# Layer 0 of a two-layer encoder: where the modulation steps stand around the start of the output projection

## The chip, the cores and the metric

The kernel runs on one core of a Trainium2 chip. The metric is the device time of one launch in microseconds (us). Each time is the median of several runs. The engines are TensorE (PE, with PEld for its weight loads), VectorE (DVE), ScalarE (ACT), GpSimd (POOL) and SyncE (SP), which issues nearly all transfers.

## What is computed

A trunk of two layers over 256 tokens of width 2048, all in 32-bit floats. In each layer a vector `c` gives six modulation vectors. The normalised input goes through one input projection whose columns feed four groups (A to D), their outputs are joined and go through the output projection `w_out`, and a gated feed-forward network follows.

```python
mod = (c_act @ w_mod[l] + b_mod[l]).reshape(bn, 6, d)
shift_m, scale_m, gate_m = mod[:, 0, None], mod[:, 1, None], mod[:, 2, None]
...
h = layer_norm(x) * (1.0 + scale_m) + shift_m
proj = h @ w_in[l]
uv, q_c, kv_c, k_r, sb, sc, sh, ag = jnp.split(proj, IN_SPLITS, axis=-1)
y_a = gmlp_mixer(...)          # A
y_b = mla_mixer(...)           # B: latent attention
y_c = short_conv_mixer(...)    # C: short convolution
y_d = conformer_conv(...)      # D: 31 taps, layer norm over channels, swish
y = jnp.concatenate([y_a, y_b, y_c, y_d], axis=-1) @ w_out[l]
x = layer_norm(ALPHA * x + (1.0 + gate_m) * y, post_mix_g[l], post_mix_b[l])
h = layer_norm(x) * (1.0 + scale_f) + shift_f
y = conv_ffn(h, ...)
x = layer_norm(ALPHA * x + (1.0 + gate_f) * y, post_ffn_g[l], post_ffn_b[l])
```

## The kernel before

**Products.** TensorE sets the time. A weight block is loaded by SP into a `raw` tile (128 x 2048 floats, 1 MB), ScalarE casts it to a high half `whi` (L414) and VectorE subtracts to get the low half `wlo` (L423), 1024 columns at a time. Three products then replace one exact product. The input projection of layer 0 and the first two units of its output projection skip the split: their weights are loaded straight into `wexact` tiles (L398), and TensorE does each of their products in two passes.

**Modulation steps.** One step is a 1 MB load of a block of `w_mod` into a `raw` tile (`wmod`, L201, on SP) and one VectorE instruction over 128 x 2048 (L205). There are 192 in all, and they need nothing but `c`, so they are strewn between the other work. `pump` does this: each unit of products adds a rate to a credit, and each whole credit draws one step. The rates stand in `RATES`, by layer and phase: `C` is the short-conv group, `out` the first chunk of the output projection, `out_next` the second, `out_tail` the first two units of the third.

**Buffers.** `wmod` and `wraw` tiles share four buffers and take them in turn. So the load of a tile waits on SP until VectorE is done with the tile four earlier, and SP issues in order: a load behind a waiting one waits too. `wexact`, `whi` and `wlo` tiles share eight others, which TensorE's products release.

**The stage around the change.** Group C of layer 0 has eight units of 1 MB, and `run` loads two units ahead, so the last two units issue no load of their own. In them `pump` still draws steps. Then the output projection (`out_proj`) takes the 2048 output columns in three chunks: 1024 (eight units u0 to u7 of 24 split products, u0 and u1 exact), 512 (four units) and 512 (four units). In the third chunk all products of token tile 0 come first, 48 of them, then 48 of tile 1. While TensorE does those of tile 1, the other engines finish and normalise tile 0 (L703 to L783, then `xn`), and TensorE turns the result (`ps_xT`, L649).

**Group D's norm** runs in between: TensorE sums the channels (`ps_mean`) and the squares (`ps_var` from `sqD`), VectorE and GpSimd make a reciprocal deviation (`rd`, L1010; L153; `dgD`, L1016), TensorE spreads it (`ps_rD`), VectorE scales `convD` by it (L1027) and ScalarE applies the swish (`yd`, L1029) and casts (`a`, L444). In layer 1 the same norm runs around the last unit of group E, just ahead of the output projection.

**Order.** The program is written as above, but the order of instructions on each engine is made by a scheduler from its own estimate of durations. So an edit of the rates also moves instructions that it does not name.

## Time and profile before

| | us |
|---|---|
| median of 3 runs | 2199.75 (2199.68 to 2200.93) |
| the profiled execution, its time | 2200.61 |
| the profiled execution, its span | 2198.8 |
| TensorE busy in the span | 2171.1 |
| VectorE busy | 1740.1 |
| ScalarE busy | 1100.8 |

The span runs from the first to the last instruction; 1.8 us lie around it. Times inside the trace count from the start of the span. Group C of layer 0 ends at about 289 us, the output projection of layer 0 runs to about 390 us, and group E of layer 1 ends at about 1361 us. A row of the timeline gives start, duration, engine, line, operation, `out<-in`, and a count of merged instructions; in brackets stands the idle time before and what ended it. A matmul's duration is its latency; how fast they follow each other is read from counts.

### The profile page before, as it was taken

The numbers are of one execution on the slowest core, as the hardware profiler recorded it, in microseconds if no ns is written. First come the engines' busy times: TensorE is split into PE (matmuls) and PEld (weight loads), VectorE is DVE, ScalarE is ACT, GpSimd is POOL, SyncE is SP. The second block draws the span as 40 slices with busy tenths as digits, with TensorE's granted clock in tenths as the row PEclk, the third lists the DMA queues.
The fourth block names the chain that finished last, engine by engine and source line by source line (L and its number), as shares of the span: only waits on it lengthen the run. The fifth ranks groups of instructions, "written<-read, shape, count | busy, mean of one in ns | idle before, by whom it ended". The sixth has DMA issues, their size and how long they took to land. (4 is left out here: it accounts for less than half of the span.)

```text
span 2198.8 us, 28486 instructions
## 1 busy us (share of the span) xinstructions
PE 2171.1 (99%) x10916; PEld 1806.8 (82%) x10916; DVE 1740.1 (79%) x2325; ACT 1100.8 (50%) x1686; POOL 21.2 (1%) x40
## 2 busy tenths in 40 slices
PE   8999999999999999999999999999999999999997
PEld 6776868688888888888868988868888888888886
DVE  5658999789889889889978989977777755565777
ACT  3133644655555455545574545465544544454553
POOL 0000000000000000000000000000000000000000
PEclk9999999999999999999999999999999999999999
DMA  9999988688999888988768647956766655565553
GB/s 390 416 377 390 366 332 335 235 333 309 331 333 338 330 330 331 358 324 286 290 230 324 206 151 294 342 218 243 262 248 246 224 190 188 189 211 192 196 197 141
DMA packets 94907, 617.08 MB, mean 281 GB/s; under 512 B 10737, under 2 KB 10929, under 8 KB 27441
## 3 DMA queue, kind: packets, MB, share of 16 engines
q1 hardware_dynamic: 94466, 614.70, 75.6%
q8 instruction: 85, 1.39, 0.2%
q0 software_dynamic: 176, 0.53, 0.1%
q14 instruction: 52, 0.43, 0.1%
q10 hardware_dynamic: 128, 0.03, 0.0%
HBM read 613.08 MB, written 2.13 MB: 280 GB/s over the span
## 5 line engine op out<-in xcount | busy, mean ns | idle before, releaser
L414 ACT CAST whi<-wraw 128x1024 fp32r<-128x1024 f32 (+1 forms) x620 | 643.8, 1046 | 683.5 <-PE g_c L121 196.0
L423 DVE TENSOR_TENSOR wlo<-wraw,whi 128x1024 fp32r<-128x1024 f32 (+1 forms) x620 | 742.9, 1213 | 278.6 <-ACT whi L414 260.8
L121 PE MATMUL v_c<-hT,whi 128*128 128x512 f32 x1408 | 489.6, 392 | 0.0
L205 DVE SCALAR_TENSOR_TENSOR wmod<-wmod,crep 128x2048 f32<-128x2048 f32 x192 | 438.4, 2286 | 60.3 <-DMA wmod<-in_w_mod_dram 59.4
L121 PE MATMUL g_c<-hT,whi 128*128 128x512 f32 x1280 | 444.6, 391 | 0.0
L121 PE MATMUL v_c<-hT,wlo 128*128 128x256 f32 x1408 | 395.1, 281 | 0.0
L121 PE MATMUL d<-whi,a 128*128 128x512 f32 x1344 | 386.7, 390 | 0.0
L121 PE MATMUL g_c<-hT,wlo 128*128 128x256 f32 x1280 | 358.8, 280 | 0.0
L121 PEld LDWEIGHTS v_c<-hT,whi 128*128 128x128 f32 x1408 | 263.8, 187 | 57.0
L121 PEld LDWEIGHTS d<-whi,a 128*128 128x128 f32 x1344 | 252.2, 188 | 52.3
L121 PEld LDWEIGHTS g_c<-hT,whi 128*128 128x128 f32 x1280 | 239.8, 187 | 51.9
L121 PEld LDWEIGHTS v_c<-hT,wlo 128*128 128x128 f32 x1408 | 266.4, 189 | 0.4 <-DVE wlo L423 0.4
L121 PEld LDWEIGHTS g_c<-hT,wlo 128*128 128x128 f32 x1280 | 242.2, 189 | 0.0
L121 PE MATMUL d<-wlo,a 128*128 128x512 f32 x672 | 233.1, 389 | 0.0
L121 PEld LDWEIGHTS d<-wlo,a 128*128 128x128 f32 x672 | 126.2, 188 | 26.2
L121 PE MATMUL o<-whi,a 128*128 128x512 f32 x416 | 120.5, 390 | 0.0
L121 PEld LDWEIGHTS o<-whi,a 128*128 128x128 f32 x416 | 77.9, 188 | 16.5 <-ACT whi L414 0.4
L448 DVE TENSOR_TENSOR a<-g,a 128x512 fp32r<-128x512 f32 x132 | 87.7, 684 | 0.0
L592 PE MATMUL first<-wexact,hN 128*128 128x512 f32 x192 | 85.5, 596 | 0.3
L444 ACT CAST a<-g 128x512 fp32r<-128x512 f32 x132 | 76.9, 614 | 0.0
L121 PE MATMUL o<-wlo,a 128*128 128x512 f32 x208 | 72.7, 393 | 1.9 <-DVE wlo L423 1.8
L1569 DVE SCALAR_TENSOR_TENSOR u<-g,par,u 128x254 f32<-128x254 f32 (+1 forms) x176 | 74.2, 477 | 0.2
(316 smaller groups left out, 2144.6 us busy)
## 6 DMA issues: line engine op xcount, KB each, us to landing
wmod<-in_w_mod_dram SPq DMA_DIRECT2D x192, 1024.0 KB, 7.1
wraw<-in_ffn_w_up_dram SPq DMA_DIRECT2D x168, 1024.0 KB, 5.4
wraw<-in_ffn_w_down_dram SPq DMA_DIRECT2D x88, 1024.0 KB, 5.0
wexact<-in_w_in_dram SPq DMA_DIRECT2D x64, 512.0 KB, 12.3
wraw<-in_w_out_dram SPq DMA_DIRECT2D x30, 1024.0 KB, 6.5
wraw<-in_w_in_dram SPq DMA_DIRECT2D x24, 1024.0 KB, 5.5
wexact<-in_ffn_w_up_dram SPq DMA_DIRECT2D x16, 512.0 KB, 5.4
wlate<-in_late_dram SPq DMA_DIRECT2D x8, 1024.0 KB, 7.1
```

The lines of the kernel that those rows point to most:

```text
L121: i = pe.matmul(o, lhsT, rhs, start=start, stop=stop, skip_group_check=True)
L205: i = dve.scalar_tensor_tensor(out=raw, in0=raw, scalar=1.0, in1=crep, op0=ALU.mult, op1=ALU.mult, accum_out=col)
L414: i = act.copy(hi[:, :m], r)
L423: i = dve.tensor_tensor(out=lo[:, :m], in0=r, in1=hi[:, :m].bitcast(F32), op=ALU.subtract)
L444: i = act.copy(hi, src)
L448: dve.tensor_tensor(out=lo, in0=src, in1=hi.bitcast(F32), op=ALU.subtract)
L592: i = pe.matmul(ps, hN[kt // 4][:, kt % 4, t * P : (t + 1) * P], parts[kt], start=kt == 0, stop=kt == KT - 1, skip_group_check=True,)
L1569: dve.scalar_tensor_tensor(out=u[:, sh:], in0=x[:, : S - sh], scalar=col(k, j), in1=u[:, sh:], op0=ALU.mult, op1=ALU.add)
```

## The change

Two edits, both on the pump. `run` sets `held` while it is in the last `ahead` units of a group, and a held pump draws nothing but keeps the credit. A pump now draws at most two steps a call. Only group C of layer 0 is run with `ahead` over 0, so only its last two units are held. The rates of layer 0's output projection are set anew: 0.75 instead of 1.0 a unit in the first chunk, 0.25 instead of 0 in the second, 1.0 instead of 0.5 in the first two units of the third.

```diff
-    dict(B=1.3, attend=1.55, C=1.9, out=1.0, out_next=0.0, out_last=0.0, out_tail=0.5, ...
+    dict(B=1.3, attend=1.55, C=1.9, out=0.75, out_next=0.25, out_last=0.0, out_tail=1.0, ...
...
     def pump():
         pace["credit"] += pace["rate"]
-        while pace["credit"] >= 1.0:
+        issued = 0
+        while pace["credit"] >= 1.0 and issued < 2 and not pace["held"]:
             pace["credit"] -= 1.0
+            issued += 1
             next(mods, None)
...
         for u in range(units):
             n = bg[u] if isinstance(bg, tuple) else bg
+            pace["held"] = u >= units - ahead
             stream(lambda: get(u), lambda item, u=u: products(item, u), n)
             pending.extend(postponed)
             postponed.clear()
+        pace["held"] = False
         pending.append(end)
```

By the rates the same number of steps is drawn by the end of the output projection: 3.8 + 8 + 0 + 1 = 12.8 credits before, 3.8 + 6 + 1 + 2 = 12.8 now. Lines behind the edits are 2 to 4 higher in the changed kernel (L414 becomes L416, L1010 becomes L1014).

**SP, from the last load of group C (`in_w_in`) to the fifth unit of the output projection.** `wmod` rows are steps, `in_w_out` rows are the output projection's weights. Before:

```order
L398 DMA wexact<-in_w_in_dram 128x1024 x2
L201 DMA wmod<-in_w_mod_dram 128x2048 x5
L398 DMA wexact<-in_w_out_dram 128x1024 x2
L201 DMA wmod<-in_w_mod_dram 128x2048
L398 DMA wexact<-in_w_out_dram 128x1024 x2
L201 DMA wmod<-in_w_mod_dram 128x2048
L403 DMA wraw<-in_w_out_dram 128x2048
L201 DMA wmod<-in_w_mod_dram 128x2048
L403 DMA wraw<-in_w_out_dram 128x2048
```

Now:

```order
L400 DMA wexact<-in_w_in_dram 128x1024 x2
L201 DMA wmod<-in_w_mod_dram 128x2048 x2
L400 DMA wexact<-in_w_out_dram 128x1024 x2
L201 DMA wmod<-in_w_mod_dram 128x2048 x2
L400 DMA wexact<-in_w_out_dram 128x1024 x2
L201 DMA wmod<-in_w_mod_dram 128x2048 x2
L405 DMA wraw<-in_w_out_dram 128x2048
L201 DMA wmod<-in_w_mod_dram 128x2048 x2
L405 DMA wraw<-in_w_out_dram 128x2048 x2
```

Two steps stand ahead of the first `w_out` load instead of five; ahead of u2's load it is six instead of seven.

**TensorE and ScalarE, where group D's norm meets the first split unit (u2).** On TensorE, before, around `ps_rD`, which stands 28 products behind `ps_var`:

```order
L121 MATMUL o_010_1657<-whi,a 128x512
L121 MATMUL o_011_1658<-whi,a 128x512
L121 MATMUL ps_rD<-dgD,ones 128x256
L121 MATMUL o_000_1655<-wlo,a 128x512
L121 MATMUL o_001_1656<-wlo,a 128x512
```

and now, with `ps_rD` directly behind `ps_var` and ahead of u2:

```order
L121 MATMUL ps_var<-ones,sqD_1677 128x1 x2
L121 MATMUL ps_var<-ones,sqD_1678 128x1 x2
L121 MATMUL ps_rD<-dgD,ones 128x256
L121 MATMUL o_000_1647<-whi,a 128x512
L121 MATMUL o_001_1648<-whi,a 128x512
L121 MATMUL o_000_1647<-wlo,a 128x512
```

ScalarE before, from the squares on:

```order
L997 ACTIVATE sqD_1681<-convD 128x512
L414 CAST whi<-wraw 128x1024 x4
L1029 ACT_TABLE_LOAD
L1029 ACTIVATE yd<-convD,par 128x256
L414 CAST whi<-wraw 128x1024 x2
L1029 ACTIVATE yd<-convD,par 128x256 x3
L444 CAST a<-yd 128x2x256 x2
```

and now:

```order
L1001 ACTIVATE sqD_1678<-convD 128x512
L1033 ACT_TABLE_LOAD
L1033 ACTIVATE yd<-convD,par 128x256
L416 CAST whi<-wraw 128x1024 x2
L1033 ACTIVATE yd<-convD,par 128x256 x3
L446 CAST a<-yd 128x2x256 x2
L446 CAST a<-ya 128x2x256 x2
L416 CAST whi<-wraw 128x1024 x18
```

The casts of u2 and u3 stood ahead of the first `yd`; now those of u2 stand behind it and those of u3 behind four casts of activations more.

**VectorE, from the deviation `rd` to the low halves of u3.** Before:

```order
L1010 TENSOR_SCALAR rd<-ps_var 128x2
L1016 TENSOR_SCALAR dgD<-cst,rd 128x128 x2
L423 TENSOR_TENSOR wlo<-wraw,whi 128x1024 x2
L205 SCALAR_TENSOR_TENSOR wmod,sums_3_1599<-wmod,crep 128x2048
L1027 TENSOR_TENSOR convD<-convD,ps_rD 128x256 x4
```

Now:

```order
L1014 TENSOR_SCALAR rd<-ps_var 128x2
L1020 TENSOR_SCALAR dgD<-cst,rd 128x128 x2
L205 SCALAR_TENSOR_TENSOR wmod,sums_3_1659<-wmod,crep 128x2048
L1031 TENSOR_TENSOR convD<-convD,ps_rD 128x256 x4
L425 TENSOR_TENSOR wlo<-wraw,whi 128x1024 x2
L205 SCALAR_TENSOR_TENSOR wmod,sums_3_1659<-wmod,crep 128x2048 x2
L450 TENSOR_TENSOR a<-yd,a 128x2x256 x2
L450 TENSOR_TENSOR a<-ya,a 128x2x256
L425 TENSOR_TENSOR wlo<-wraw,whi 128x1024 x2
```

Before, u2's low halves were done ahead of `rd` and u3's stand in the shown rows directly behind `dgD`; now both stand behind the norm, and two steps and three subtractions of activations separate them.

Two more places move. In the third chunk seven of tile 1's products now stand among the last of tile 0's, so 41 of tile 1's 48 are left behind tile 0's last one; there VectorE has one step more, between `tlo` and `wlo`, and the two small instructions that prepare the norm's constants (L730, L741) stand behind the first `yg` instead of ahead of it. In layer 1, in the last unit of group E, the first two `ps_var` products stand behind 10 of the 16 high products instead of 13, and ScalarE casts two weight tiles and then takes both squares, where it took one square between the two casts.

## Rows read from the trace of the kernel before

**Rows 1.** The page, busy time of the engines.

```profile
PE 2171.1 (99%) x10916; PEld 1806.8 (82%) x10916; DVE 1740.1 (79%) x2325; ACT 1100.8 (50%) x1686; POOL 21.2 (1%) x40
```

**Rows 2.** TensorE's waits: total us, times, longest; whole span.

```profile
PE o L121 <- DMA wexact<-in_w_out_dram: 2.9, 1, 2.9
PE o L121 <- DVE wlo L423: 1.8, 3, 1.4
```

**Rows 3.** Stretches: length, busy (count) of PE, PEld, DVE, ACT, POOL, clock, DMA share, GB/s.

```profile
286.00:309.30 23.30, 20.41 (x71) 11.85 (x70) 22.15 (x32) 6.51 (x11) 0.00 (x0) 1.00 0.89 342
309.30:337.00 27.70, 26.09 (x112) 20.36 (x112) 26.20 (x32) 13.48 (x18) 0.70 (x1) 1.00 0.95 366
...
337.00:367.60 30.60, 30.36 (x135) 24.82 (x133) 30.40 (x35) 15.80 (x16) 0.00 (x0) 1.00 0.87 327
```

**Rows 4.** Timeline of TensorE, end of group C to the first split unit.

```profile
288.99 1.89 PE L121 MATMUL ps_mean<-convD,ones 128*128 128x256 f32 x8
293.77 14.00 PE L121 MATMUL o<-wexact,ya 128*128 128x512 f32 x32 [2.89 <-DMA wexact<-in_w_out_dram]
307.61 1.84 PE L121 MATMUL ps_var<-ones,sqD 128*128 128x1 f32 x16
309.31 0.72 PE L121 MATMUL o<-whi,a 128*128 128x512 f32 x2
311.39 0.73 PE L121 MATMUL o<-wlo,a 128*128 128x512 f32 x2 [1.36 <-DVE wlo L423]
```

**Rows 5.** Timeline of SP's issues, end of group C to u2.

```profile
270.40 17.38 SPq L201 DMA_DIRECT2D wmod<-in_w_mod_dram  x5
287.87 0.86 SPq L398 DMA_DIRECT2D wexact<-in_w_out_dram  x2
...
273.00 10.35 SPq L201 DMA_DIRECT2D wmod<-in_w_mod_dram  x3
```

**Rows 6.** Timeline of VectorE, GpSimd and ScalarE around group D's norm.

```profile
307.90 2.29 DVE L205 SCALAR_TENSOR_TENSOR wmod<-wmod,crep 128x2048 f32<-128x2048 f32 x1
310.11 2.36 DVE L423 TENSOR_TENSOR wlo<-wraw,whi 128x1024 fp32r<-128x1024 f32 x2
...
314.59 0.16 DVE L1010 TENSOR_SCALAR rd<-ps_var 128x2 f32<-128x2 f32 x1
315.63 0.48 DVE L1016 TENSOR_SCALAR dgD<-cst,rd 128x128 f32<-128x128 f32 x2 [0.88 <-POOL rd L153]
...
320.51 1.41 DVE L1027 TENSOR_TENSOR convD<-convD,ps_rD 128x256 f32<-128x256 f32 x4
...
320.97 0.60 ACT L1029 ACTIVATE yd<-convD,par 128x256 f32<-128x256 f32 x1 [5.37 <-DVE convD L1027]
321.47 1.98 ACT L414 CAST whi<-wraw 128x1024 fp32r<-128x1024 f32 x2
...
332.71 1.29 DVE L448 TENSOR_TENSOR a<-ya,a 128x512 fp32r<-128x512 f32 x2
```

**Rows 7.** Timeline of the third chunk: tile 0's end and the turned result.

```profile
378.68 0.69 DVE L703 TENSOR_TENSOR yg<-o,gate 128x512 f32<-128x512 f32 x1 [2.76 <-PE o L121]
...
389.76 1.36 PE L649 MATMUL ps_xT<-cst,xn 128*128 128x128 f32 x8 [0.24 <-ACT xn L126]
```

**Rows 8.** Timeline of layer 1, last unit of group E.

```profile
1352.98 3.31 PE L121 MATMUL E_c<-hT,whi 128*128 128x512 f32 x13
1354.62 1.05 ACT L414 CAST whi<-wraw 128x1024 fp32r<-128x1024 f32 x1 [9.37 <-DMA wraw<-in_w_out_dram]
1355.58 0.62 ACT L997 ACTIVATE sqD<-convD 128x512 f32<-128x512 f32 x1
1356.26 0.61 PE L121 MATMUL ps_var<-ones,sqD 128*128 128x1 f32 x4
```

**Rows 9.** Stretches at the end of the span, columns as in rows 3.

```profile
2188.00:2190.00 2.00, 0.00 (x0) 0.00 (x0) 1.90 (x5) 0.00 (x0) 0.00 (x0) 1.00 0.00 0
2190.00:2192.00 2.00, 0.00 (x0) 0.00 (x0) 2.00 (x4) 0.00 (x0) 0.90 (x1) 0.59 0.00 0
```

More of the change, by code (lines that the diff above doesn't have):

```diff
@@ L35 @@
 RATES = [
-    dict(B=1.3, attend=1.55, C=1.9, out=1.0, out_next=0.0, out_last=0.0, out_tail=0.5, up_first=0.5, up_late=0.75, up_renewed=0.75, up_third=0.6, up=0.75, down=0.7, down_next=0.45, down_last=0.3, down_tail=0.5),
+    dict(B=1.3, attend=1.55, C=1.9, out=0.75, out_next=0.25, out_last=0.0, out_tail=1.0, up_first=0.5, up_late=0.75, up_renewed=0.75, up_third=0.6, up=0.75, down=0.7, down_next=0.45, down_last=0.3, down_tail=0.5),
     dict(D=1.0, U=0.0, V=0.0, B=0.0, C=0.0, E=1.35, attend=0.0, out=0.75, out_next=0.6, out_last=0.0, out_tail=0.0, up_first=0.3, up_late=0.3, up_renewed=0.3, up_third=0.3, up=0.3, down=0.7, down_next=0.7, down_last=0.0, down_tail=0.0),
@@ L323, in encoder_kernel @@
     )
-    pace = {"rate": 0.0, "credit": 0.0, "phase": None}
+    pace = {"rate": 0.0, "credit": 0.0, "phase": None, "held": False}
     def phase(l, name):
```

## The prediction

> **What bounds the kernel now.** I read the page's busy times first. TensorE is busy 2171.1 of 2198.8 us, 99% [rows 1], so an edit can only win time at a place where TensorE stands still, and loses whatever stops it anew. The profiled execution took 2200.61 us, 0.86 us over the median of 2199.75 us; I make the sum as a difference and put it on the median. TensorE's waits come next: around the change they are one wait of 2.9 us for the first `w_out` load and 1.8 us in three waits for `wlo` [rows 2]. That is all that a better order can win there, 4.7 us. Third, the stretches: from 286 to 309.3 us VectorE is busy 22.15 of 23.3 us, and from 309.3 to 367.6 us it is busy 56.6 of 58.3 us [rows 3]. VectorE has almost no slack, so where an instruction stands in its queue decides when TensorE gets it. Fourth, the timelines of each engine around the norm of group D, from which the terms are taken.
>
> **Term 1, the load that comes sooner.** SP issues five steps between 270.40 and 287.87 us; each waits for a buffer, and the first `w_out` load waits behind them, so it goes out only at 287.87 us [rows 5]. TensorE starts its products at 293.77 us, after 2.89 us of waiting [rows 4]. Issue to use is 293.77 - 287.87 = 5.9 us. Now only two steps stand ahead. With the third step of before, at 273.00 us [rows 5], the load could go out some 15 us sooner, and it is needed at 290.9 us. The wait goes: **-2.9 us**. What TensorE meets next at that spot are 32 products and 16 small ones whose other operands were long there.
>
> **Term 2, the norm of group D without cover.** This is the largest. `ps_var` ended at 309.31 us [rows 4], and 2.89 us sooner is 306.42 us. Before, 28 products of the split units stood between `ps_var` and `ps_rD`, and the chain between the two ran beside them. Now `ps_rD` stands directly behind, so the chain is naked. VectorE is free by then: what it has ahead of `rd` is 15.9 us of work after 289.9 us, that is until 305.7 us (four steps at 2.21 us, start to start 307.90 to 310.11 [rows 6], and 7.0 us of the same small instructions as before). From `rd` at 306.5 us, GpSimd's part and both `dgD` take 314.59 to 316.11 in the trace, 1.52 us [rows 6], so `ps_rD` starts at 308.2 us: a wait of 1.8 us. Its own two passes are work that it had before too, at 0.24 us each like the products of the same shape in `ps_mean` (1.89 us for 8 [rows 4]): until 308.65 us.
>
> Then u2's high products want `whi`. ScalarE's cast now stands behind the first `yd`, that behind the first `convD`, and that, on VectorE, behind a step put between `dgD` and `convD`. VectorE: `dgD` ends at 308.04, the step at 310.25. The first `convD` to the first `yd` is 320.51 to 320.97, 0.46 us; the `yd` to the cast is 0.50 us, and a cast is 1.98 / 2 = 0.99 us [rows 6]: 310.25 + 0.46 + 0.50 + 0.99 + 0.1 = 312.3 us. TensorE waits 3.65 us more. Together **+5.5 us**. Nothing else that TensorE has stands ahead of these products in its queue, so nothing hides it; from below the term is bound by the 1.52 us of the bare chain.
>
> **Term 3, u2's low half.** TensorE waited 1.36 us for it [rows 4]. Now both engines are released by the same cast at 312.2 us; from the start of the `wlo` at 310.11 us to its product at 311.39 us it took 1.28 us, and two products cover 0.5 us of that: a wait of 0.8 us, **-0.6 us**.
>
> **Term 4, u3's low half.** Behind u2's two `wlo` (from 312.3, start to start 2.27 us) VectorE now has two steps (4.42 us) and three subtractions of activations (half of 1.29 us, about 0.6 us each [rows 6]) before u3's first `wlo`: start at 320.8 us, usable at 322.1 us. TensorE gets there after 26 products. One product takes 30.60 / 135 = 0.2267 us [rows 3], so it arrives at 313.6 + 5.9 = 319.5 us. **+2.5 us**, bounds 0 (if these subtractions or a step stood aside) and 4.
>
> **Term 5, the small waits of before.** From 311.39 to 367.60 us TensorE took 56.2 us [rows 3, 4]. The two stretches count 247 products; without `ps_rD`'s two passes, u2's first two and the last of `ps_var` some 238 are left, and they and `ps_rD` need 238 x 0.2267 + 0.45 = 54.4 us, so 1.8 us were lost in small pieces, which fits the 1.85 us by which busy falls short of the stretches. After the delays of terms 2 and 4, loads and low halves are ahead of TensorE there. I take **-1.2 us**, between 0 and -1.8.
>
> **Term 6, the step in the third chunk.** One step more (2.21 us) stands on VectorE ahead of a `wlo` of tile 0. VectorE would finish that tile at about 377.0 us when TensorE wants it at about 376.3. **+0.6 us**, between 0 and 2.2.
>
> **Term 7, the cover of tile 0's norm.** From the end of tile 0 (378.64 us, `yg` starts at 378.68) to the turned result takes 389.76 - 378.64 = 11.1 us; tile 1's 48 products hid all but 0.24 us of it [rows 7] (48 x 0.2267 = 10.9). Seven of these products now stand ahead. The 41 left cover 9.3 us, and the two small instructions that stand behind the first `yg` lengthen the chain by some 0.4 us. Wait 11.1 + 0.4 - 9.3 = 2.2 us, **+1.9 us**. The seven are not lost, but they fill no hole at their new place. Bounds 0 (if they fill term 6's wait, and the small ones cost nothing) and 2.2.
>
> **Term 8, layer 1.** The scheduler reorders the last unit of group E too. TensorE's first 13 high products start at 1352.98 us; `ps_var` follows at 1356.26 us, 0.3 us later than they end. Now 10 stand ahead, until 1355.25 us. The squares stand behind two casts instead of one: 1354.62 + 2 x 0.98 + 0.62 = 1357.2 us, and `ps_var` at 1357.3 us [rows 8]. Wait 2.0 instead of 0.3, **+1.7 us**, at least 0.7 if the three products moved behind fill a later gap. In its new place the `ps_rD` there has enough products before it.
>
> **Sum:** -2.9 + 5.5 - 0.6 + 2.5 - 1.2 + 0.6 + 1.9 + 1.7 = +7.5 us. 2199.75 + 7.5 = **2207.2 us**. With single terms at their bounds the sum goes from about +5 to +10; I keep 2204.7 to 2209.7 us for this case.
>
> **The rivals.**
>
> *The clock falls in the new wait.* The granted clock stood at 1.00 through the stretch that holds the 2.9 us wait [rows 3]. At the end of the span, where TensorE has nothing left to do, it was still 1.00 from 2188 to 2190 us and 0.59 from 2190 to 2192 us [rows 9], so an idle TensorE does lose its clock, and the new wait of 3.65 us, with 1.8 us just ahead of it, is longer than any around the change. Products at 1.2 GHz take double their 0.2267 us. If u2's 24 products ran so, they would take 5.4 us more; 2.5 us of that is term 4's wait anyway, so 0 to 3 us come on top: 2207 to 2210 us. The Trainium skill ("TensorE: Matmul & The Clock Gate", Part 1, HAM oscillation) says that a kernel whose TensorE waits for transfers between tiles gets every following tile at the lower clock; by that rule this would be the likelier case, while the wait of 2.9 us here shows no fall. Chance 0.12.
>
> *The later terms come out at their lower ends.* Terms 4 to 8 rest on my walk along VectorE's queue, with hand-overs of some tenths. With term 4, 6 and 7 at 0, term 5 at -1.8 and term 8 at 0.7, the sum is -2.9 + 5.5 - 0.6 - 1.8 + 0.7 = +0.9 us. Half of the way there is +4.2. For it: each wait gives VectorE time to catch up. Against: VectorE's new queue holds two steps just where u3 needs it. 2200.5 to 2204.1 us, 2203 us as its middle. Chance 0.20.
>
> *The other side: VectorE sets the pace.* VectorE is busy 97% of the first chunk [rows 3]. Two steps (4.4 us) leave it before the third chunk. If VectorE rather than TensorE decides when the first chunk ends, TensorE's new wait at u2 is made good behind it: -2.9 of term 1 and all of the 1.8 us of term 5 remain, 2195.0 us, or 2196.9 us with term 1 alone. It decides itself at u2: the high half must be there by about 309 us and not by 312.3. Against it: TensorE's idle time from 309.3 to 367.6 us is 1.85 us in all, which can't give back 5.5 us. Chance 0.07.
>
> *The change does not do what it says.* The `w_out` load has two steps ahead still, and each needs a buffer that VectorE releases; if the load still goes out near 287 us, the 2.9 us stay, and the sum is +10.4 us, 2210.2 us. Chance 0.05.
>
> **How the numbers follow.** The forecast has the remaining 0.56. The least that a measurement of this kernel can tell from no change is about 0.2%, 4.4 us. The forecast, the clock and the failed load lie over 2204.15 us: slower 0.73. The lower ends and most of the other side lie within: same 0.24. Faster needs nearly all of the 4.7 us that there are to win: 0.03. For the range I leave out the other side (0.07), the lower part of the second rival (0.05) and the top of the clock's and the failed load's (0.06): 2201.5 to 2210.3 us.
>
> **What would show it.** In the profile after: TensorE's wait for `w_out` is gone and the issue of that load lies before 280 us (term 1). Behind `ps_var`, a wait on `dgD` of 1.8 us and one on `whi` of about 3.7 us, the largest new one (term 2). Waits on `wlo` of about 0.8 and 2.5 us (terms 3 and 4). Before `ps_xT` of layer 0 a wait on `xn` of about 2.2 us (term 7), and in layer 1 one on `sqD` of about 2.0 us (term 8). TensorE's busy time stays at 2171 us; if it rises by over 2 us with a granted clock under 1.00 near 312 us, the clock rival holds. If the wait on `whi` is under 1 us, the forecast is wrong from the ground up, since then VectorE's step and the norm's chain lie ahead of `ps_var`.

## The result and the profile after

The changed kernel takes 2206.14 us (median of 11 runs, 2204.99 to 2216.09) beside 2200.30 us for the kernel before on the same chip. The ratio is 1.0029, 95% interval 1.0016 to 1.0042: slower, by about 6 us. The forecast was 2207.2 us (2201.5 to 2210.3). The profiled execution took 2205.77 us with a span of 2204.0 us, 5.2 us over the span of before; the terms below are held against these 5.2 us. In the set of the four experiments from the second covered norm to the filler at the turned result, 14 of 34 executions of the kernel before took 2204.7 to 2211.2 us and the others 2199.7 to 2202.4 us (two far off, at 3675.7 and 7085.4 us, are left out), so the spans of the profiles are given beside the ratios.

The busy times of the changed kernel answer to [rows 1]. TensorE is at 2173.6 us instead of 2171.1 us, the two other large engines within 2.1 us of where they were:

```profile
PE 2173.6 (99%) x10916; PEld 1807.5 (82%) x10916; DVE 1741.5 (79%) x2325; ACT 1102.9 (50%) x1686; POOL 22.1 (1%) x40
```

TensorE's waits over the whole span of the changed kernel answer to [rows 2] (what it waits for; total us, times, longest):

```profile
PE o L121 <- ACT whi L416: 2.9, 1, 2.9
PE ps_xT L653 <- ACT xn L126: 2.4, 3, 1.9
PE ps_rD L121 <- DVE dgD L1020: 1.8, 2, 1.6
...
```

The wait of 2.9 us for `w_out` is gone. In its place stand one on `whi`, one on `dgD`, one on `xn` and (0.5 us, in the rows of layer 1 below) one on `sqD`, each at the place the prediction named. SP's timeline shows why the load is in time: it goes out at 273.70 us, 14.2 us sooner than in [rows 5], behind two steps.

```profile
270.68 2.93 SPq L201 DMA_DIRECT2D wmod<-in_w_mod_dram  x2
273.70 0.86 SPq L400 DMA_DIRECT2D wexact<-in_w_out_dram  x2
```

TensorE's timeline of the changed kernel around the norm of group D, the answer to [rows 4]:

```profile
291.00 13.90 PE L121 MATMUL o<-wexact,ya 128*128 128x512 f32 x32
304.73 1.84 PE L121 MATMUL ps_var<-ones,sqD 128*128 128x1 f32 x16
308.19 1.22 PE L121 MATMUL ps_rD<-dgD,ones 128*128 128x256 f32 x2 [1.62 <-DVE dgD L1020]
312.30 1.22 PE L121 MATMUL o<-whi,a 128*128 128x512 f32 x2 [2.89 <-ACT whi L416]
...
322.06 0.72 PE L121 MATMUL o<-wlo,a 128*128 128x512 f32 x2 [0.48 <-DVE wlo L425]
```

Read downwards: the exact products start 2.8 us sooner than before, then TensorE stands behind `ps_var`, does two passes, stands again until u2's high half is there, and meets u3's low half at 322.06 us. VectorE and ScalarE in the same stretch, the answer to [rows 6]:

```profile
306.61 0.16 DVE L1014 TENSOR_SCALAR rd<-ps_var 128x2 f32<-128x2 f32 x1 [0.56 <-PE ps_var L121]
307.65 0.48 DVE L1020 TENSOR_SCALAR dgD<-cst,rd 128x128 f32<-128x128 f32 x2 [0.88 <-POOL rd L153]
308.04 2.29 DVE L205 SCALAR_TENSOR_TENSOR wmod<-wmod,crep 128x2048 f32<-128x2048 f32 x1
310.25 1.41 DVE L1031 TENSOR_TENSOR convD<-convD,ps_rD 128x256 f32<-128x256 f32 x4
...
311.22 1.98 ACT L416 CAST whi<-wraw 128x1024 fp32r<-128x1024 f32 x2
```

The step at 308.04 us stands between `dgD` and `convD`, and the cast stands behind that: that is the wait of 2.89 us.

One thing the busy times hide: TensorE's clock fell. Stretches of the changed kernel (from:to, length; busy us and count of PE, PEld, DVE, ACT, POOL; granted clock; DMA share; GB/s):

```profile
304.70:307.20 2.50, 1.87 (x17) 1.75 (x15) 1.51 (x3) 0.00 (x0) 0.29 (x1) 1.00 0.55 200
307.20:312.30 5.10, 1.22 (x3) 0.50 (x3) 4.04 (x9) 1.59 (x3) 0.41 (x1) 0.50 0.72 222
312.30:317.10 4.80, 4.76 (x10) 3.30 (x11) 4.80 (x5) 4.80 (x9) 0.00 (x0) 0.50 0.74 265
317.10:318.20 1.10, 1.10 (x5) 0.90 (x4) 1.10 (x1) 1.10 (x2) 0.00 (x0) 0.84 0.99 417
```

0.50 is the lower of the clock's two levels, 1.2 GHz. It holds from 307.2 us into the stretch that begins at 317.1 us; the ten products recorded from 312.3 to 317.1 us fill 4.8 us, where at full clock a product takes 0.23 us.

Farther on, the third chunk ([rows 7]) and layer 1 ([rows 8]) of the changed kernel, on TensorE's timeline, with ScalarE's first casts of layer 1:

```profile
394.06 1.36 PE L653 MATMUL ps_xT<-cst,xn 128*128 128x128 f32 x8 [1.88 <-ACT xn L126]
395.27 3.70 PE L594 MATMUL first<-wexact,hN 128*128 128x512 f32 x8
...
1355.34 1.89 PE L121 MATMUL ps_mean<-convD,ones 128*128 128x256 f32 x8
1356.88 2.63 PE L121 MATMUL E_c<-hT,whi 128*128 128x512 f32 x10
1357.41 2.00 ACT L416 CAST whi<-wraw 128x1024 fp32r<-128x1024 f32 x2 [8.24 <-DMA wraw<-in_w_out_dram]
1359.99 0.60 PE L121 MATMUL ps_var<-ones,sqD 128*128 128x1 f32 x4 [0.49 <-ACT sqD L1001]
...
1365.10 0.70 PE L121 MATMUL ps_rD<-dgD,ones 128*128 128x256 f32 x2 [0.23 <-DVE dgD L1020]
```

The same points in both traces, as start times:

| point on TensorE | before | after | later by |
|---|---|---|---|
| `ps_mean` of layer 0 | 288.99 | 289.27 | 0.28 |
| first exact product of `w_out` | 293.77 | 291.00 | -2.77 |
| first product of u2 | 309.31 | 312.30 | 2.99 |
| last product of tile 1 | 389.13 | 391.79 | 2.66 |
| turned result, `ps_xT` | 389.76 | 394.06 | 4.30 |
| `ps_mean` of layer 1 | 1351.44 | 1355.34 | 3.90 |
| first product of layer 1's output projection | 1360.75 | 1366.11 | 5.36 |
| end of the span | 2198.8 | 2204.0 | 5.2 |

### The profile page after: what moved, and what is told of

The parts are those of the page before. It is cut to its first block, busy times and chain, and to the rows that moved or that the text cites. A ratio compares the mean times of both kernels' runs of the same rounds, so it can differ in the third digit from the quotient of the medians.

```text
span 2204.0 us, 28481 instructions
## 1 busy us (share of the span) xinstructions
PE 2173.6 (99%) x10916; PEld 1807.5 (82%) x10916; DVE 1741.5 (79%) x2325; ACT 1102.9 (50%) x1686; POOL 22.1 (1%) x40
## 5 line engine op out<-in xcount | busy, mean ns | idle before, releaser
L416 ACT CAST whi<-wraw 128x1024 fp32r<-128x1024 f32 (+1 forms) x620 | 645.4, 1047 | 693.7 <-PE g_c L121 200.6
```

The costliest lines, as they stand in the source:

```text
L416: i = act.copy(hi[:, :m], r)
```

## The experiments

Ratios are to the kernel before, run on the same chip, with a 95% interval.

**The change in halves.** First the hold and the cap of two with the rates of before (against the changed kernel):

```diff
-    dict(... out=0.75, out_next=0.25, out_last=0.0, out_tail=1.0, ...
+    dict(... out=1.0, out_next=0.0, out_last=0.0, out_tail=0.5, ...
```

> The changed kernel with the rates of before: only the hold in the last two units and the cap of two a call are left. Theory (the norm without cover): the order at the norm and in layer 1 is that of the changed kernel, so TensorE still waits 1.6 us for dgD and 2.9 us for whi, and loses 1.3 us in layer 1; only the wait before ps_xT goes, since all 48 products of tile 1 stand behind tile 0 again. That is 1.6 us under the changed kernel: +4.2 us to the kernel before, ratio 1.0019 (1.0010 to 1.0024). Rival (the steps moved by the rates are what costs): the hold alone is neutral or gains the 2.9 us of the w_out wait, ratio 0.9987 to 1.0003.

Measured: 1.0018 (1.0009 to 1.0027). TensorE's waits at the norm of group D are those of the whole change (1.62, 2.89 and 0.46 us), and the turned result has next to no wait (0.23 us, at 392.75 us). In layer 1 the clock fell to 0.59 (1362 to 1366 us), and `ps_mean` to the first product of the output projection took 12.06 us, where the whole change takes 10.77. The span of the profile is 2203.6 us.

Then the new rates without hold and cap (against the kernel before):

```diff
-    dict(... out=1.0, out_next=0.0, out_last=0.0, out_tail=0.5, ...
+    dict(... out=0.75, out_next=0.25, out_last=0.0, out_tail=1.0, ...
```

> The kernel before with the new rates alone, no hold and no cap. Theory (the norm without cover): ps_rD keeps its 28 products of cover and layer 1 its old order, the wait of 2.9 us for w_out stays, and the only loss is the cover of tile 0's norm, a wait of about 1.9 us before ps_xT: +1.7 us to before, ratio 1.0008 (1.0003 to 1.0012). Together with the other run the two parts should add up to the changed kernel's +5.8 us. Rival (the moved steps cost): ratio 1.0020 to 1.0030 here, as the changed kernel.

Measured: 1.0007 (0.9999 to 1.0016), span 2200.8 us; the interval just holds no change. By the medians the halves cost 4.1 and 1.7 us, together 5.8 us; the whole change costs 5.8 us (2206.14 - 2200.30). So by the medians the two halves add up, and some seven tenths come from the hold with its cap. In the profiles they don't: the spans are 4.8 and 2.0 us over that of before, 6.8 us together, where the whole change has 5.2. Each half's trace has a fall of the clock that the whole's lacks, the first half's in layer 1 and the second half's behind the turned result. The sum of the medians is no proof, then, that the whole is made of these two parts. The trace of the second half, TensorE around the turned result,

```profile
389.63 1.36 PE L649 MATMUL ps_xT<-cst,xn 128*128 128x128 f32 x8 [1.89 <-ACT xn L126]
390.84 5.40 PE L592 MATMUL first<-wexact,hN 128*128 128x512 f32 x8
```

and the stretch there:

```profile
390.80:394.06 3.26, 3.26 (x7) 1.30 (x6) 3.12 (x7) 3.26 (x9) 0.95 (x1) 0.57 0.71 292
```

It brought the turned result 0.13 us sooner than before in spite of a wait that is 1.65 us longer [rows 7]: most of the small waits of the chunks (term 5's 1.8 us) was gone. The loss came behind it: eight products at 5.40 us instead of 3.70 us, with the clock at 0.57. So the ratio of my theory came out by another way than the one I gave, and that is luck. In the whole change the same wait (1.88 us) stands there too, and the eight products take 3.70 us. So one wait of one length was followed by the lower clock in one trace and not in the other.

**What does the lower clock at u2 cost?** Products that nothing reads keep TensorE busy: three between `ps_var` and `ps_rD`, seven between `ps_rD` and u2.

```diff
+                if l == 0:
+                    for _ in range(3):
+                        i = mm(box["r"][:, S : 2 * S], ones, cosT, True, True)
...
+                if l == 0:
+                    fill = ms_tile("fill")
+                    for _ in range(7):
+                        j = mm(fill[:, :S], ones, cosT, True, True)
...
```

> The changed kernel with ten products whose result nothing reads: three between ps_var and ps_rD and seven between ps_rD and u2, each two passes of 0.24 us, so that TensorE is at work where it waited 1.6 and 2.9 us, and no other engine's queue changes. Theory (the lower clock is hidden in what follows): the granted clock is 1.00 from 306 to 318 us where it was 0.50 from 307.2 to 317.1, u2's products take 5.4 us again, and TensorE then waits some 2.5 us for u3's first wlo at 322.1 us instead of 0.5. Time as the changed kernel's within 0.5 us, ratio to before 1.0027 (1.0022 to 1.0031). Rival (the clock costs time of its own): 2 to 3 us under the changed kernel, ratio 1.0013 to 1.0018.

Measured: 1.0036 (1.0022 to 1.005), span of the profile 2203.6 us. The ratio lies over the range that I gave. It is that of five executions, two at 2204.4 and 2205.3 us (the profiled one) and three from 2209.1 to 2210.5 us; what sets the three apart has no trace, so the reading rests on the profile. TensorE's timeline,

```profile
308.55 0.70 PE L121 MATMUL ps_rD<-dgD,ones 128*128 128x256 f32 x2 [0.21 <-DVE dgD L1021]
309.09 3.19 PE L121 MATMUL fill<-cst,ones 128*128 128x256 f32 x14
312.67 1.21 PE L121 MATMUL o<-whi,a 128*128 128x512 f32 x4 [0.39 <-ACT whi L416]
...
322.43 0.73 PE L121 MATMUL o<-wlo,a 128*128 128x512 f32 x2 [2.77 <-DVE wlo L425]
```

and the stretch there:

```profile
310.00:318.00 8.00, 7.56 (x33) 5.72 (x32) 7.39 (x11) 6.92 (x12) 0.00 (x0) 1.00 0.70 224
```

The clock stays at 1.00, TensorE does u2 at full speed, and then waits 2.77 us for u3's low half instead of 0.48 us, which it uses at 322.43 instead of 322.06 us. The 0.37 us between the two were there ahead of the filler: `ps_var` starts at 305.09 instead of 304.73 us. The slow products of the changed kernel filled a wait that TensorE would have had anyway. Nothing was won.

**Can the cover be put back?** VectorE's `rd` is ordered behind u2's low halves and `ps_rD` behind u3's products, and the first chunk draws one step a unit at most.

```diff
-        while pace["credit"] >= 1.0 and issued < 2 and not pace["held"]:
+        while pace["credit"] >= 1.0 and issued < (1 if pace["phase"] == "out" else 2) and not pace["held"]:
...
+                if l == 0:
+                    tc.add_manual_dep(i.ins, unit_low[2], order_dep, reason="the unit's low halves come first")
...
+                if l == 0:
+                    tc.add_manual_dep(i.ins, unit_end[3], order_dep, reason="the unit's products come first")
```

> The changed kernel with the norm covered: ps_rD is ordered behind the last product of u3 and rd behind u2's second wlo, and at most one step is drawn a unit in the first chunk, so that no step stands between the squares and u2's wlo. Theory (the norm without cover): the waits for dgD, whi and u3's wlo (5.3 us, with the half clock) go, and the 2.9 us for w_out stay gone. Left are the loss in layer 1 (1.3 us) and a wait before ps_xT of some 1.3 us, since 44 products of tile 1 stand behind tile 0. Against before -3.0 - 1.4 - 0.4 + 1.1 + 1.3 = -2.4 us, ratio 0.9989 (0.9980 to 1.0000). Rival (VectorE sets the pace of the first chunk): its queue is as full as before, and TensorE waits for wlo of the later units instead; ratio 1.0005 to 1.0025.

Measured: 1.0021 (1.0012 to 1.003); the theory fell, its rival held. u2 starts at 306.18 us with no wait, but I had put `ps_rD` too late. The timeline of VectorE, and farther on of TensorE:

```profile
317.84 0.42 DVE L1037 TENSOR_TENSOR convD<-convD,ps_rD 128x256 f32<-128x256 f32 x1 [3.71 <-PE ps_rD L121]
...
352.34 0.79 PE L121 MATMUL o<-wlo,a 128*128 128x512 f32 x1 [3.62 <-DVE wlo L425]
```

VectorE stood still for 3.71 us, and 35 us later TensorE waited 3.62 us for VectorE. I took the one for the cause of the other, and the next kernel tests that.

So next the same without that idle time: `ps_rD` behind u2's products, the first `convD` behind u3's low half.

```diff
-                    tc.add_manual_dep(i.ins, unit_end[3], order_dep, reason="the unit's products come first")
+                    tc.add_manual_dep(i.ins, unit_end[2], order_dep, reason="the unit's products come first")
...
+                    if l == 0 and j == 0:
+                        tc.add_manual_dep(i.ins, unit_low[3], order_dep, reason="the unit's low halves come first")
```

> The covered norm again, with ps_rD behind the last product of u2 instead of u3, and the first convD behind u3's wlo. In the covered version VectorE stood idle for 3.7 us at 314 us until ps_rD came, and TensorE waited 3.6 us for a wlo of the second chunk at 352 us. Theory (VectorE is the bound behind the norm, and its idle time comes back as TensorE's wait): VectorE's idle time goes, TensorE's waits for wlo fall from 5.5 us to under 2.5, and the time falls by 3 to 3.7 us against the covered version: ratio to before 1.0006 (0.9998 to 1.0010). Rival (the wait at 352 us comes from the two steps drawn at the start of the second chunk, whatever VectorE did before): the wait stays at over 3 us, ratio 1.0018 to 1.0024.

Measured: 1.0007 (0.9992 to 1.0022), span 2200.7 us, 3.3 us under the changed kernel's and under that of the covered version. The time is the theory's, the sign in the trace is the rival's: VectorE's idle time is gone, but TensorE's waits for `wlo` fall only from 5.5 to 3.8 us, and the largest stays. Its product starts at 349.82 instead of 352.34 us, so of the 3.71 us 2.5 came back there. No wait is left from the first product of `w_out` to 340 us. One is left in the second chunk, and the timeline of VectorE and TensorE shows what is ahead of it:

```profile
341.07 2.28 DVE L205 SCALAR_TENSOR_TENSOR wmod<-wmod,crep 128x2048 f32<-128x2048 f32 x1
...
344.47 2.29 DVE L205 SCALAR_TENSOR_TENSOR wmod<-wmod,crep 128x2048 f32<-128x2048 f32 x1
...
348.55 2.35 DVE L425 TENSOR_TENSOR wlo<-wraw,whi 128x1024 fp32r<-128x1024 f32 x2
...
349.82 0.80 PE L121 MATMUL o<-wlo,a 128*128 128x512 f32 x1 [3.68 <-DVE wlo L425]
```

Two steps drawn together at the start of the second chunk, 4.4 us of VectorE, make a wait of 3.7 us. In the next kernel all three chunks draw one step a unit at most, and the third draws none of its own.

```diff
-        while pace["credit"] >= 1.0 and issued < (1 if pace["phase"] == "out" else 2) and not pace["held"]:
+        while pace["credit"] >= 1.0 and issued < (1 if pace["phase"].startswith("out") else 2) and not pace["held"]:
...
-    dict(... out_tail=1.0, ...
+    dict(... out_tail=0.0, ...
```

> As the run with the covered norm and no idle VectorE, with at most one step a unit in all three chunks and none in the third, so that one step fewer than before the change and two fewer than now are drawn ahead of tile 0's norm; they come in the feed-forward network instead, where VectorE is busy 75 to 90% of the time. Theory (VectorE's work in the three chunks sets what the load that comes sooner is worth): all 48 products of tile 1 stand behind tile 0 again, the wait before ps_xT is under 0.5 us, the waits for wlo are under 2 us, and only layer 1's 1.3 us are left of the losses: ratio 0.9993 (0.9982 to 1.0002). Rival (the steps cost as much wherever they stand): ratio 1.0004 to 1.0012.

Measured: 1.0008 (0.9993 to 1.0022), span 2202.9 us, 4.1 us over that of before; the gain was missed. The trace shows that it was made first: the turned result starts at 385.33 us, 4.4 us sooner than before, and the second one at 1124.25 us, 4.8 us sooner. Then it was lost in layer 1. Two steps fewer had been drawn by the end of the output projection; the gate that needs them all draws the missing ones where it stands, in the norm of layer 1's tile 0. The timeline of TensorE and VectorE there,

```profile
1446.92 1.97 PE L653 MATMUL ps_xT<-cst,xn 128*128 128x128 f32 x8 [2.46 <-ACT xn L126]
...
1447.94 2.29 DVE L205 SCALAR_TENSOR_TENSOR wmod<-wmod,crep 128x2048 f32<-128x2048 f32 x1 [1.92 <-DMA wmod<-in_w_mod_dram]
...
1451.05 3.78 PE L594 MATMUL first<-wexact,hN 128*128 128x512 f32 x4 [2.17 <-ACT hN L126]
```

and the stretches there (the kernel before has a clock of 1.00 in both):

```profile
1440.00:1450.00 10.00, 6.42 (x28) 4.94 (x26) 7.16 (x15) 3.15 (x6) 0.56 (x1) 0.84 0.85 332
1450.00:1460.00 10.00, 8.95 (x20) 4.72 (x21) 8.31 (x21) 8.54 (x22) 0.99 (x1) 0.65 0.52 161
```

**What is the cap of two worth?** The changed kernel without it: the kept credit of the held units is drawn at once.

```diff
-        while pace["credit"] >= 1.0 and issued < 2 and not pace["held"]:
+        while pace["credit"] >= 1.0 and not pace["held"]:
```

> The changed kernel without the cap of two a call, so that four steps are drawn in one call behind u0's loads. TensorE's order then has ps_var ahead of the eight products of u1, and ps_rD behind them. Theory (the cap is what keeps VectorE's queue short at the norm): four steps (8.8 us) stand among the centring of convD, so the squares come only near 305 us and TensorE, done with u0 near 298 us, waits some 7 us ahead of ps_var; the eight products then cover the chain to ps_rD, so the waits for dgD and whi (4.5 us) go, and u2 starts about 2.4 us later than in the changed kernel. Half of that is taken up where u3's wlo made TensorE wait, and a fall of the clock would add to it: ratio to before 1.0035 (1.0025 to 1.0055). Rival (the cap is neutral): 1.0027.

Measured: 1.0045 (1.0029 to 1.006), span 2208.7 us, 4.7 us over the changed kernel's. The kept steps stand among the small instructions that centre `convD`, and TensorE waits 4.58 and 1.95 us for the squares:

```profile
302.01 1.02 PE L121 MATMUL ps_var<-ones,sqD 128*128 128x1 f32 x4 [4.58 <-ACT sqD L1001]
```

u2 starts at 317.67 us, 5.4 us later than in the changed kernel, where 2.4 had been forecast: the clock was at 0.50 from 302 to 312 us, and u1's sixteen products took 10.04 us.

**The lower clock behind the turned result.** The new rates alone, with four products that nothing reads ahead of `ps_xT`.

```diff
+        if (l, m_shift, t, q) == (0, SHIFT_F, 0, 0):
+            behind = last_mm[0]
+            for _ in range(4):
+                i = mm(ps[:, :S], ones, cosT, True, True)
```

> The run with the new rates alone, plus four products that nothing reads (1.9 us) in TensorE's wait before ps_xT of tile 0. In that run the granted clock was 0.50 to 0.60 from 390.8 to 394.1 us, behind a wait of 1.9 us, and the first eight products on the normalised tile took 5.4 us instead of 3.7. Theory (here nothing hides the lower clock): the clock stays at 1.00, these products take 3.7 us, and 1.7 us come back: ratio to before 0.9999 (0.9993 to 1.0004). Rival (the clock falls in few executions only, and what the rates cost is the wait itself): no change, ratio 1.0007.

Measured: 1.0006 (0.9989 to 1.0022), span 2200.3 instead of 2200.8 us. The interval holds both expectations; the times decide nothing. The trace does. TensorE's timeline at the first `w_out` products and behind the turned result,

```profile
294.62 15.52 PE L121 MATMUL o<-wexact,ya 128*128 128x512 f32 x32 [2.67 <-DMA wexact<-in_w_out_dram]
...
392.03 3.70 PE L592 MATMUL first<-wexact,hN 128*128 128x512 f32 x8
```

and the stretch at the former:

```profile
294.00:298.00 4.00, 3.38 (x5) 1.56 (x6) 4.00 (x6) 0.00 (x0) 0.00 (x0) 0.57 1.03 411
```

Behind the filler the clock stays at 1.00, and the eight products take 3.70 us as the theory had it. From the first turned block to the second it takes 395.57 - 390.82 = 4.75 us, and 396.07 - 389.63 = 6.44 without the filler: 1.7 us came back. They don't show in the span because this execution had lost 1.2 us at 213 us, in the attention's products, where the clock fell too (24 products of `ps_qn` at 6.67 instead of 5.45 us). And the clock fell a second time, behind the wait for `w_out`. That wait is 2.67 us in the run without the filler too, and there the clock stayed at 1.00. This fall cost nothing: the exact products took 1.5 us longer (15.52 instead of 14.00 us), and the wait of 1.58 us for u2's low half, which the run without the filler has, was gone.

**Where can the two steps stand that the kernel with the steps later owes?** First in the third group of the up projection (`up_third` 0.6 to 0.85).

```diff
-    dict(... up_third=0.6, ...
+    dict(... up_third=0.85, ...
```

> The run with the steps later, and the two missing steps repaid in the third group of the feed-forward network of layer 0 (rate 0.85 instead of 0.6). In that run TensorE reached ps_xT at 385.3 us, 4.4 us ahead of the kernel before, and lost it all in layer 1, where two steps were forced between the parts of tile 0's norm (waits of 2.5 and 2.2 us at 1447 and 1451 us, and the clock at 0.65 to 0.84 behind them). Theory: with as many steps drawn by then as before the change, these waits go, the repaid steps are hidden (VectorE is busy 44 of 50 us there), and -4.4 + 1.3 for layer 1's order = -3.1 us are left: ratio to before 0.9986 (0.9977 to 0.9996). Rival (the repaid steps cost there what they cost in the output projection): ratio 0.9995 to 1.0008.

Measured: 1.0001 (0.9992 to 1.001); the forecast was missed, the rival's range holds it. The steps are on time, and the norm of layer 1 has its wait of before again (0.23 us). But the gain was gone by the second turned result: 385.35 and 1130.72 us, where before had 389.76 and 1129.08. The trace has no wait between them. A stretch of the up projection, in which TensorE is busy throughout:

```profile
520.00:700.00 180.00, 180.00 (x1021) 156.12 (x1020) 164.68 (x216) 92.49 (x137) 0.00 (x0) 1.00 0.91 333
```

There are 1021 products in 180 us. The kernel before has 1038 recorded there, the changed one and the one with the steps later 1040, all at a clock of 1.00. From 520 to 880 us it is 2046 against 2079 before, 1.6%, and 1.6% of 360 us is some 6 us: what was lost. The number of steps alone does not explain it: from 560 to 880 us VectorE does 43 steps here and 44 in the kernel before.

In the same set stood two kernels that order layer 1's squares ahead of the two casts (term 8): the last one with that order, and the changed kernel with it alone.

```diff
+            if (l, k0, c0, width, k) == (1, 0, 0, 1024, 0):
+                tc.add_manual_dep(i.ins, squares[0], order_dep, reason="the squares come first")
...
+                    squares[b] = i.ins.name
```

> The same with one order more in layer 1: the first cast of w_out's first unit on ScalarE behind the first square of group D's norm, so that the square does not wait behind two casts whose load lands late. Theory: layer 1's loss of 1.3 us falls to 0.5 or less, -3.1 - 0.8 = -3.9 us to before: ratio 0.9982 (0.9973 to 0.9992). Rival (the loss in layer 1 comes from the three high products that moved behind ps_var, not from the casts): as the run without it, 0.9986.

> The changed kernel with that one order in layer 1 and nothing else. Theory: TensorE's wait of 0.5 us for sqD and that of 0.2 us for dgD in layer 1 go, and the time from ps_mean to the first product of w_out there falls from 10.8 us to 10.0 or less (9.6 before the change with ps_rD added): -0.8 us to the changed kernel, ratio to before 1.0023 (1.0017 to 1.0028). Rival: no change, 1.0027.

Measured: 1.0003 (0.9994 to 1.0012), the forecast missed, again with 1021 products in those 180 us, and 1.0020 (1.0011 to 1.0028), span 2203.2 us. The latter ran on the same chip and has 1040 products there, so the chip is not what sets them apart. In it the wait for the squares is gone. From `ps_mean` to the first product of layer 1's output projection it takes 1365.49 - 1355.52 = 9.97 us, where the changed kernel takes 1366.11 - 1355.34 = 10.77 and the kernel before 1360.75 - 1351.44 = 9.31. So the order of those casts is 0.8 us of term 8.

Last, the two steps in layer 0's down projection instead (`down` 0.7 to 0.8, `up_third` at 0.6 again).

```diff
-    dict(... up_third=0.85, up=0.75, down=0.7, ...
+    dict(... up_third=0.6, up=0.75, down=0.8, ...
```

> The order of the kernel in which all three chunks of layer 0's output projection draw one step a unit at most (it ends that projection 4.4 us sooner than before and pays for the two missing steps inside layer 1's norm), with the two steps drawn in layer 0's down projection instead of the third group of its up projection. Where they stood in the up projection the gain was gone between the two turned results, 385.35 and 1130.72 us, against 389.76 and 1129.08 before: its products stood 1.7% farther apart (1021 against 1038 records in the 180 us from 520 us on), with no wait in the record. Theory A, that loss belongs to the place: turned results at 385.3 and 1124.6 us (before: 1129.08), layer 1 as before with its norm 0.7 us dearer, ratio 0.9983 (0.9976 to 0.9993), faster than both kernels. Rival, wherever two more steps stand VectorE is late for the low halves and TensorE slows: second turned result at 1127 to 1131 us, ratio 0.9995 to 1.0010.

Measured: 0.9985 (0.9976 to 0.9994), 2198.82 us beside 2201.03: faster than the kernel before, by 0.15%, and by the two ratios 0.4% faster than the changed one. TensorE's timeline of it,

```profile
386.62 1.36 PE L653 MATMUL ps_xT<-cst,xn 128*128 128x128 f32 x8 [0.30 <-ACT xn L126]
...
1125.53 1.36 PE L653 MATMUL ps_xT<-cst,xn 128*128 128x128 f32 x8 [0.29 <-ACT xn L126]
...
1347.88 1.89 PE L121 MATMUL ps_mean<-convD,ones 128*128 128x256 f32 x8
...
1353.51 0.60 PE L121 MATMUL ps_var<-ones,sqD 128*128 128x1 f32 x4 [1.47 <-ACT sqD L1003]
```

and four stretches, of layer 0's attention, of the up projection and of layer 1:

```profile
212.00:216.00 4.00, 4.00 (x12) 2.92 (x11) 3.80 (x4) 3.14 (x9) 0.00 (x0) 0.63 1.03 408
...
520.00:700.00 180.00, 180.00 (x1041) 158.72 (x1040) 164.50 (x219) 97.13 (x141) 0.00 (x0) 1.00 0.90 334
...
1356.00:1358.00 2.00, 2.00 (x10) 1.78 (x10) 1.29 (x2) 1.04 (x1) 1.50 (x1) 0.62 0.58 246
1358.00:1360.00 2.00, 2.00 (x12) 1.95 (x10) 1.93 (x3) 0.00 (x0) 0.04 (x1) 0.52 0.76 197
```

The up projection runs at its old pace, and the lead of 3.1 us at the turned result is 3.6 us at `ps_mean` of layer 1. (It was 4.4 us in the kernel with the steps later; the 1.3 us between them went in the attention's products at 213 us, where the clock fell to 0.63, and `ps_mean` of layer 0 came at 289.98 instead of 288.71 us.) There most of it goes: 1.47 us in the wait for the squares and some 1.6 us in the lower clock behind it (`ps_mean` to the first product of the output projection takes 12.8 us, 9.3 before, 0.4 of it the passes of `ps_rD` that now stand ahead). In this execution, which took 2200.0 us, 0.6 us are left at the end of the span; the median is 1.2 us below it. The mean granted clock on record says that not every execution has these falls: four at 0.998 and 0.999 took 2196.2 to 2196.9 us, a fifth at 0.998 took 2203.85 us, and the six at 0.996 and 0.997, the profiled one among them, took 2198.3 to 2200.0 us. The two falls cost 1.3 and 1.6 us in the trace, which fits the difference; but only the profiled execution has a trace, so this is likely and not shown. The ratio is the one that was forecast, while layer 1, forecast 0.7 us dearer, is some 3.1 us dearer in this execution. The order of the squares was not tried in this kernel.

## Why the prediction was right, point by point

The sign, the place of each large new wait and the time of the whole were right; the sum of the terms was 2.3 us too high against the profiled execution (+7.5 against +5.2 us).

| term | forecast | measured | from |
|---|---|---|---|
| 1, the `w_out` load | -2.9 | -3.05 | table above: -2.77 - 0.28 |
| 2, the naked norm | +5.5 | +5.3 | 2.99 + 2.77 - 0.45 (two passes of `ps_rD`) |
| 3 to 6, to the end of tile 1 | +1.3 | +0.1 | 2.66 - 2.99 + 0.45 |
| 7, tile 0's norm | +1.9 | +1.6 | 4.30 - 2.66 |
| to layer 1 | 0 | -0.4 | 3.90 - 4.30 |
| 8, layer 1 | +1.7 | +1.1 | 5.36 - 3.90 - 0.35 (passes of `ps_rD`, now ahead) |
| ahead of the first point and behind the last | 0 | +0.5 | 0.28, and 5.2 - 5.36 + 0.35 |

**Term 1** held: the load goes out well before 280 us. The rival that it might still go out near 287 us is out.

**Term 2** held to a tenth: `ps_rD` was forecast for 308.2 us and starts at 308.19, u2 for 312.3 and starts at 312.30. The walk along VectorE's queue (the step between `dgD` and `convD`, then `yd`, then the cast) is the chain of the trace. Only the split differs: the two passes themselves ran at the lower clock, 1.22 us, so the wait on `whi` reads 2.89 instead of 3.65 us.

**Terms 3 and 4** held in their effect and not in their form. u3's low half was forecast to be usable at 322.1 us and is used at 322.06, but TensorE waits 0.48 us for it and not 2.5, because it came late through u2 at the lower clock. With the clock held up the wait is 2.77 us: the forecast's mechanism, uncovered by an experiment. Term 3's own wait of 0.8 us for u2's low half did not come either: u2's first two products took 1.22 us at the lower clock and covered it.

**The clock rival** was given 0.12 and described as costing 0 to 3 us on top. By the sign that the prediction set for it (busy time up by over 2 us, a clock under 1.00 near 312 us) it holds: 2173.6 instead of 2171.1 us, and 0.50. So the forecast's own case, a busy time that stays at 2171 us, did not happen. The lower clock cost the lower end of what the rival had said, nothing, and the time, 2206.14 us, lies under the rival's 2207 to 2210 us. The prediction had seen that 2.5 us of it were term 4's wait anyway; what it had not seen is how likely the fall is. I had weighed the long wait of [rows 3], at which the clock stayed up, as the nearest row. That was one execution: behind a wait of 2.67 us at the same place the clock fell to 0.57 in the trace of the new rates with the filler. The trace says that waits of 1.62 and 2.89 us with two passes between them are not that case: the clock was down at 307.2 us already, before TensorE had stood still for a whole microsecond.

**Terms 5 and 6** are where half of the excess lies. From 322.06 us to the last product of tile 1 TensorE has no wait at all: term 5 is -1.8 us and not -1.2, its lower bound, and term 6 is 0 and not +0.6, also its lower bound. Behind two delays VectorE was ahead everywhere. That is the second rival (the later terms at their lower ends) in part: it was right on terms 5 and 6, and wrong on terms 4 and 7.

**Term 8** had the mechanism right, with the size too large. The casts' load landed about 1 us sooner relative to TensorE than assumed (the first two casts start at 1357.41 us, 2.07 us behind `ps_mean`; before, the first started at 1354.62 us [rows 8], 3.18 us behind it), so the wait for the squares is 0.49 us and not 2.0. The rest of the 1.1 us stands in the new place of `ps_var` and `ps_rD`, and 0.8 us of it goes with the order of the casts.

**VectorE as the pace-maker** (the other side, 0.07) was wrong for the changed kernel, whose delay at u2 isn't given back. But the experiments show the same engine as the bound of the stretch once TensorE's waits there are taken away: with 3.71 us of VectorE's idle time gone, the product that waited for it came 2.5 us sooner.

**Layer 0's own gain is real but small.** The two waits that the change could win are 4.7 us [rows 2], and the kernel with the steps later wins 4.4 of them at the turned result. What was left in the end differs with the place to which the steps went that it no longer did there: in layer 1's norm the gain was lost (ratio 1.0008), in the up projection as well (1.0001), in the down projection some of it stayed (0.9985). Why the products of the up projection stand 1.6% farther apart in the two kernels that pay there, with no wait in the trace, as many steps in most of the stretch and a granted clock of 1.00, is open.

## What to carry to other kernels

Before a wait of the busiest engine is taken away, look at what other chain ran beside the work behind it: here the load's wait of 2.9 us went, and a norm that 28 products had covered stood bare for 5.3 us. Work that is moved off a crowded stretch has to be followed to the place where it is due: here it had to be drawn one piece at a time and by the time that its reader needs it, and which stretch takes it at no cost was found only by trying. A lower clock costs only what the next wait would not have taken anyway, so price it up to that wait and not beyond.

## What was not expected of the hardware

TensorE's clock does not follow the length of a wait alone. It stayed at 1.00 across the 2.89 us before the exact products in the kernel before [rows 3, 4], and across 1.88 us before `ps_xT` in the changed kernel. It was at 0.50 from 307.2 us in the changed kernel, when TensorE had done sixteen `ps_var` products of one column each and then stood still for under 1 us, and at 0.57 behind 1.89 us before `ps_xT` with the new rates alone, and at 0.62 and 0.52 behind 1.47 us in layer 1 of the last kernel. In the first of these falls it came back only some 10 us later (307.2 to the stretch from 317.1 us), 6 us of which TensorE was at work.

Nor does it follow the order of instructions alone. Behind the same wait of 2.67 us for `w_out` it stayed at 1.00 with the new rates and fell to 0.57 with the new rates and the filler. From 212 to 216 us, where TensorE does the same products in each of these kernels behind waits of under 0.4 us, it was 1.00 before and in the changed kernel, and 0.57, 0.57 and 0.63 in three of the others (the filler at u2, the filler at the turned result, and the last kernel). A single trace, with or without a fall, doesn't tell what the next execution does; what decides it was not found.
